# Third sum two pairs of steps sooner, standard chunks kept apart, activation sums in three steps, first loads one by one

## The chip, the cores and the metric

The kernel runs on one core of one Trainium2 chip. The metric is the device time of one execution in microseconds (us). The median of three runs before the change is 2226.44 us, from 2221.94 to 2226.76.

## What is computed

A block of a streaming encoder, float32, 256 frames of 2048 channels: half an FFN, two token mixers side by side (attention over chunks and retention) with gates, half an FFN again, and a final norm. The FFNs are the part that this change touches.

```python
def rmsnorm(x, g):
    y = x * lax.rsqrt(jnp.mean(x * x, axis=-1, keepdims=True) + EPS)
    return y * g

def swiglu_ffn(x, w_gate, w_up, w_down):      # 2048 -> 5632 -> 2048
    return (jax.nn.silu(x @ w_gate) * (x @ w_up)) @ w_down

x = x + 0.5 * swiglu_ffn(rmsnorm(x, g1), w1_gate, w1_up, w1_down)
...
x = x + merged @ w_out
x = x + 0.5 * swiglu_ffn(rmsnorm(x, g2), w2_gate, w2_up, w2_down)
return rmsnorm(x, norm_final_g)
```

## The kernel before

**One product in three matmuls.** Every float32 operand is split into hi (rounded to the matmul's own format, a copy on ACT, line 119) and lo (the rest, a subtraction on DVE, line 120). `three` (lines 127 to 129) adds hi x hi, hi x lo and lo x hi into one PSUM bank. A matmul has 128x128 weights and 512 columns.

**Steps.** The whole program is a list of steps, written out when the kernel is built. A standard step (a "chunk", `standard`) takes 2 x 128 rows of one weight matrix by 512 columns: SP loads 512 KB into one of 4 raw tiles, ACT and DVE split them, and PE does 12 matmuls (2 row blocks x 2 halves of the frames x 3). `run` emits for step c first the preparation (`prep`) of up to four steps ahead of it, then what `later` has made due at step c, then the products of step c. Engines are in order, so this order of emission is the order on each engine; they wait for each other by semaphores alone, and an engine with nothing to wait for runs ahead of the others.

**The groups.** In each FFN, 2 of the 11 blocks of 512 hidden columns are done with standard steps (`plain`), the other 9 as a `Strassen` group, which computes gate and up of one block with seven half-size products in place of eight. It works on sums: x and k are tiles of 512 KB that POOL's queue loads (line 495; at most 8 at a time, `KEPT`), x from gate's weights and k from up's. A group has four phases with four positions jc each. Phases 0, 1 and 2 have pairs of half steps ("r", of a plain tile, and "s", of a sum), phase 3 has four single half steps; a half step has 6 matmuls. In order:

- phase 0: x += k (DVE, line 526); split k (r), then x (s)
- phase 1: SP loads a raw tile of gate; x += raw (line 531); split raw (r), then x (s)
- phase 2: SP loads a raw tile of up; k = x - k (the third sum, line 533); POOL issues a transfer that adds a tile of up's weights to x while it writes (the accumulating transfer, line 534, 512 KB); split raw (r), then k (s)
- phase 3: split x (s)

Once k is prepared in phase 2 and x in phase 3, their room goes to the next group's loads, which POOL's queue issues in between. Groups are named in the trace by the number of their first step: z12, z51, z89, z128, z166, z205, z243, z281, z320 in the first FFN and z624, z663, z701, z740, z778, z817, z855, z893, z932 in the second. A tile's name has the phase, the position and r or s at the end: `hiz16633s` is hi of z166, phase 3, jc 3, sum.

**Chunks between the half steps.** The order is made in `ffn`. After a lead of 12 chunks, groups run in sequence, and every pair (a quarter of it for the singles of phase 3) adds `rate`, about 0.80, to a credit. While the credit is at least 0.6 (0.2 at the end of a phase) a chunk of the queue follows, if what it reads is at hand. So there are mostly three or four chunks in a phase and one in phase 3. Where a job had to wait for its input, the credit grows over 1 and two chunks follow each other: six times in each FFN. Most chunks are of `down`, where each job's banks are first seeded with x on ACT (line 673) and emptied on ACT (line 676); two of those six double chunks go across from one such job to the next.

**The activations.** `Norm.put` transposes x and splits it. For the groups, `add_up` makes four further sums (s5, s6, s3, s7) for each half of the channels: DVE adds into a tile n1f or n2f (lines 444 to 453), then ACT makes hi (line 407) and DVE lo (408). They are due 1, 3, 5 and 7 steps after the last `put` of the half. 1/rms is made of the squares by DVE (line 336) and POOL (line 337); SiLU of the first plain block (f1g, f2g, line 635) needs it.

**Other work that lies in POOL's queue.** The bias table of the attention (biasT, line 313) is loaded 24 steps ahead of the mixers' first step, that is within phase 2 of z320; PE turns it (psb, line 323) four steps later.

Of the kernel before, what the change touches and what calls it, by code (L numbers as in the profile page):

```python
# [8 lines left out]
F32 = mybir.dt.float32  # L9
F32R = mybir.dt.float32r  # L10
AF = mybir.ActivationFunctionType
ALU = mybir.AluOpType
# [15 lines left out]
KC = 2  # L28
# [9 lines left out]
HALF_K = D // P // 2  # L38
LEAD = 12
SINGLE = 0.25  # L40
HELD = 6
PLAIN = (9, 10)
PASSES = ((9, 0), (10, 1), (2, 3), (4, 5), (6,), (7,), (8,))
WARM = (6, 3)
# [24 lines left out]
def block_kernel(ctx: ExitStack, tc: tile.TileContext, x, g1, w1g, w1u, w1d, gm, w_in, rel, woa, wor, wo,  # L69
                 g2, w2g, w2u, w2d, gf, cos, sin, decay, ident, out):  # L70
    nc = tc.nc
# [23 lines left out]
    steps = []  # L95
    transfers = []
    kept = []
# [4 lines left out]
    def later(n, fn):  # L102
        due.setdefault(state["step"] + n, []).append(fn)
# [4 lines left out]
    def chunk(w, r0, c0):  # L108
        return w[r0 : r0 + KC * P, c0 : c0 + NB].rearrange("(k p) n -> p k n", p=P)
# [5 lines left out]
    def split(raw, name, parts=(slice(0, KC),)):  # L115
        hi = wpool.tile([P, KC, NB], F32R, tag="hi", bufs=SPLIT_BUFS, name=f"hi{name}")
        lo = wpool.tile([P, KC, NB], F32R, tag="lo", bufs=SPLIT_BUFS, name=f"lo{name}")
        for p in parts:
            nc.scalar.copy(hi[:, p, :], raw[:, p, :])  # L119
            nc.vector.tensor_sub(lo[:, p, :], raw[:, p, :], hi[:, p, :].bitcast(F32))  # L120
        return hi, lo
# [250 lines left out]
    class Norm:  # L372
# [25 lines left out]
                if self.sums:  # L398
                    nc.vector.tensor_scalar_mul(self.minus, self.rstd, -1.0)

        def split_to(self, key, js, src):
            if key not in self.part:
                self.part[key] = [
                    apool.tile([P, HALF_K, P], F32R, tag="act", name=f"{self.name}{key}{i}") for i in "hl"
                ]
            hi, lo = self.part[key]
            nc.scalar.copy(hi[:, js, :], src)
            nc.vector.tensor_sub(lo[:, js, :], src, hi[:, js, :].bitcast(F32))

        def put(self, b, half):  # L410
            if half == 0:
                self.raw[b] = act_tile(F32, f"{self.name}x{b}")
            raw = self.raw[b]
            ps = side_tile(f"{self.name}p{b}{half}")
            for i in range(2):
                k = 4 * b + 2 * half + i
                for t in range(NT):
                    nc.tensor.transpose(
                        ps[:, (2 * i + t) * P : (2 * i + t + 1) * P], xs[t][:, k * P : (k + 1) * P], id_sb
                    )  # L420
            for i in range(2):
                k = 4 * b + 2 * half + i
                nc.scalar.activation(
                    raw[:, 2 * half + i, :], ps[:, i * SEQ : (i + 1) * SEQ], AF.Copy, scale=self.gain[:, k : k + 1]
                )
            j = 4 * (b // 2) + 2 * half
            for t in range(NT):
                src = raw[:, 2 * half : 2 * half + 2, t * P : (t + 1) * P]
                self.split_to(f"a{t}{b % 2}", slice(j, j + 2), src)
            if half == 1 and not self.sums:  # L430
                del self.raw[b]
            elif half == 1 and b % 2 == 1:
                for i, key in enumerate(self.SUMS):
                    later(1 + 2 * i, lambda key=key: self.add_up(b // 2, key))

        def add_up(self, p, key):

            a11, a21, a12, a22 = [self.raw[2 * p + i][:, :, t * P : (t + 1) * P] for i in range(2) for t in range(NT)]
            if key == "s5":
                f = act_tile(F32, f"{self.name}f{p}").rearrange("p a (h q) -> p h a q", h=2)  # L440
                self.f[p] = f[:, 0], f[:, 1]
            f0, f1 = self.f[p]
            if key == "s5":
                nc.vector.tensor_sub(f0, a22, a21)
                src = f0
            elif key == "s6":
                nc.vector.scalar_tensor_tensor(f1, f0, -1.0, a11, op0=ALU.mult, op1=ALU.subtract)
                src = f1
            elif key == "s3":
                nc.vector.scalar_tensor_tensor(f0, f1, -1.0, a12, op0=ALU.mult, op1=ALU.subtract)  # L450
                src = f0
            else:
                nc.vector.tensor_sub(f1, a11, a21)
                src = f1
                del self.raw[2 * p], self.raw[2 * p + 1], self.f[p]
            self.split_to(key, slice(4 * p, 4 * p + 4), src)

        def __call__(self, k, t):
            b = k // 4
# [12 lines left out]
    class Strassen:  # L472
# [37 lines left out]
        def step(self, phase, jc, of_sum):  # L510
            made = {}
            name = f"{self.name}{phase}{jc}{'rs'[of_sum]}"
            n = HALF_K // KC

            def load():
                made["raw"] = weights_tile(f"raw{name}")
                i = 2 - phase
                fetch(made["raw"], self.w[i], self.rows(1, jc), self.col[i])

            def prep():  # L520
                x = self.x[jc]
                if not of_sum:

                    k = self.kept[jc]
                    if phase == 0:
                        nc.vector.tensor_add(x, x, k)
                        made["w"] = split(k, name)
                        return
                    raw = made.pop("raw")
                    if phase == 1:  # L530
                        nc.vector.tensor_add(x, x, raw)
                    else:
                        nc.vector.tensor_sub(k, x, k)
                        nc.gpsimd.dma_start(x, chunk(self.w[0], self.rows(1, jc), self.col[0]), accum_op=ALU.add)
                    made["w"] = split(raw, name)
                elif phase == 2:
                    made["w"] = split(self.kept.pop(jc), name)
                elif phase == 3:
                    made["w"] = split(self.x.pop(jc), name)
                else:  # L540
                    made["w"] = split(x, name)

            bank, form, fresh, closing = {
# [4 lines left out]
            }[phase, of_sum]  # L548

            def products():  # L550
                hi, lo = made["w"]
                if fresh and jc == 0:
                    self.bank(bank)
                for i in range(KC):
                    three(
                        self.acc[bank], self.norm.form(form, KC * jc + i), (hi[:, i, :], lo[:, i, :]),
                        fresh and jc == 0 and i == 0, closing and jc == n - 1 and i == KC - 1, True,
                    )
                if jc == n - 1:
                    self.end(phase, of_sum)  # L560

            loaded = not of_sum and phase in (1, 2)
            frees = ["raw"] if loaded else ["kept"] if of_sum and phase > 1 else []
            return Step(self, 0, load if loaded else None, prep, frees, products)
# [53 lines left out]
    def ffn(name, norm, wg, wu, wd, after):  # L618
# [70 lines left out]
        first, second = [plain(b) for b in PLAIN]  # L689
# [8 lines left out]
        def next_standard():  # L698

            job, k = queue[0]  # L700
            if len(queue) <= apart or any(at_hand.get(b, len(steps) + 1) > len(steps) for b in job.needs):
                return False
            steps.append(standard(job, k))
            del queue[0]
            if job.makes is not None and k + KC == job.nk:
                at_hand[job.makes] = len(steps) + 5
            return True

        for _ in range(LEAD):
            next_standard()  # L710
        groups = [b for b in range(nblocks) if b not in PLAIN]
        pairs = 3 * (HALF_K // KC)
        rate = (len(queue) - apart) / (len(groups) * (pairs + SINGLE * HALF_K // KC))
        credit = 0.0
        for b in groups:
            group = paired(b)
            kept.extend((len(steps) - 10 if b == groups[0] else 0, fn) for fn in group.loads())
            for i, part in enumerate(group.steps()):
                steps.extend(part)
                credit += rate * (1 if i < pairs else SINGLE)  # L720
                if i + 1 == pairs + HALF_K // KC:
                    at_hand[b] = len(steps) + 6
                while credit >= (0.2 if (i + 1) % (HALF_K // KC) == 0 else 0.6) and next_standard():
                    credit -= 1
        for job, k in queue:
            steps.append(standard(job, k))
# [286 lines left out]
    def at(step, fn):  # L1013
        due.setdefault(step, []).append(fn)
# [119 lines left out]
```

## Time and profile before

| what | us |
|---|---|
| median of 3 runs | 2226.44 |
| the profiled execution | 2227.66 |
| its span, first to last instruction | 2225.9 |
| nine groups of the first FFN (66.4 to 743.5) | 677.1 |
| mixers and the projection after them (743.5 to 1483.5) | 740.0 |
| nine groups of the second FFN (1520.9 to 2173.9) | 653.0 |

The profile page gives busy time and share of the span for each engine (PE is TensorE, PEld its weight loads, DVE VectorE, ACT ScalarE, POOL GpSimd; SPq and POOLq are the queues that issue transfers). Rows of the table by stretches have the stretch and its length, then busy us with the count of instructions for PE, PEld, DVE, ACT and POOL, then the granted clock of TensorE (1 is full), the busy share of the 16 DMA engines, and GB/s. Rows of a timeline have start, duration, engine, source line, operation, tiles as out<-in, and in brackets how long the engine was idle before it and what ended that. Rows of waits have who waited for whom: total us, times, longest.

### The profile page before, as it was taken

How to read it: one execution, taken by the hardware profiler on the slowest of the kernel's cores; microseconds unless marked ns; L12 is line 12 of the kernel's file. 1: busy time of each engine (PE TensorE's matmuls, PEld its weight loads, DVE VectorE, ACT ScalarE, POOL GpSimd, SP SyncE). 2: the span in 40 equal slices, each digit the busy share in tenths (PEclk: the TensorE clock that was granted, in tenths of full speed). 3: DMA queues.
4: the chain of work that ended last, by engine and by line, in shares of the span. 5: the costliest groups of instructions: out<-in, count | busy, mean ns of one | idle time of the engine just before them, and what ended most of it. 6: DMA issues, size and time to landing. Idle time of an engine off the chain costs nothing.

```text
span 2225.9 us, 25616 instructions
## 1 busy us (share of the span) xinstructions
PE 2127.7 (96%) x9376; PEld 1730.3 (78%) x9376; DVE 1629.9 (73%) x1678; ACT 1325.5 (60%) x1648; POOL 215.2 (10%) x252
## 2 busy tenths in 40 slices
PE   7998999999999899999999999999999999999998
PEld 5776877787778788888888888887778777877786
DVE  4987988898888554555665554568889888888886
ACT  6565666676667664455444444556666566766675
POOL 1012101110111000000000000010111011101200
PEclk9999999999999999999999999999999999999999
DMA  7479657866786656656556666565787578767874
GB/s 256 120 230 284 193 181 234 263 189 191 232 249 170 200 177 183 189 163 178 170 161 191 192 194 190 187 231 159 227 265 207 173 227 254 201 191 223 263 193 147
DMA packets 214669, 452.27 MB, mean 203 GB/s; under 512 B 14016, under 2 KB 14768, under 8 KB 214544
## 3 DMA queue, kind: packets, MB, share of 16 engines
q1 hardware_dynamic: 172256, 331.39, 47.9%
q0 software_dynamic: 42144, 119.19, 18.9%
q8 instruction: 73, 1.20, 0.2%
q14 instruction: 52, 0.43, 0.1%
q10 hardware_dynamic: 144, 0.07, 0.0%
HBM read 446.92 MB, written 3.67 MB: 202 GB/s over the span
## 4 chain that ended last, share of the span: by engine, by line
PE 59%; issue 13%; DMA 11%; DVE 7%; ACT 7%; POOL 2%; ACTq 0%; SPq 0%; POOLq 0%; DVEq 0%
PE acc L128 15%; PE acc L129 15%; PE acc L127 15%; DVE lo L120 2%; ACT hi L119 2%; DMA raw<-in_ffn_w_down_dram 1%; DMA raw<-in_ffn_w_gate_dram 1%; DMA z205x<-in_ffn_w_gate_dram 1%; DMA z855x<-in_ffn_w_gate_dram 1%; DMA z663x<-in_ffn_w_gate_dram 1%; DMA z243x<-in_ffn_w_gate_dram 1%; DMA z740x<-in_ffn_w_gate_dram 1%; DMA z51k<-in_ffn_w_up_dram 1%; DMA gf<-in_norm_final_g_dram 1%; DMA z51x<-in_ffn_w_up_dram 1%
## 5 line engine op out<-in xcount | busy, mean ns | idle before, releaser
L120 DVE TENSOR_TENSOR lo<-raw,hi 128x1024 fp32r<-128x1024 f32 (+1 forms) x481 | 584.7, 1221 | 397.0 <-ACT hi L119 394.9
L119 ACT CAST hi<-raw 128x1024 fp32r<-128x1024 f32 (+1 forms) x481 | 503.1, 1049 | 357.1 <-PE acc L129 305.9
L127 PE MATMUL acc<-hi,nma00h 128*128 128x512 f32 x176 | 70.6, 401 | 0.0
L127 PE MATMUL acc<-hi,nma01h 128*128 128x512 f32 x176 | 70.1, 398 | 0.0
L129 PE MATMUL acc<-hi,nma00l 128*128 128x512 f32 x176 | 68.7, 390 | 0.0
L129 PE MATMUL acc<-hi,nma01l 128*128 128x512 f32 x176 | 68.6, 390 | 0.0
L127 PE MATMUL acc<-hi,nma10h 128*128 128x512 f32 x176 | 68.6, 390 | 0.0
L128 PE MATMUL acc<-lo,nma00h 128*128 128x512 f32 x176 | 68.6, 390 | 0.0
L128 PE MATMUL acc<-lo,nma01h 128*128 128x512 f32 x176 | 68.6, 390 | 0.0
L127 PE MATMUL acc<-hi,nma11h 128*128 128x512 f32 x176 | 68.6, 390 | 0.0
L129 PE MATMUL acc<-hi,nma10l 128*128 128x512 f32 x176 | 68.6, 390 | 0.0
L129 PE MATMUL acc<-hi,nma11l 128*128 128x512 f32 x176 | 68.6, 390 | 0.0
L128 PE MATMUL acc<-lo,nma10h 128*128 128x512 f32 x176 | 68.5, 389 | 0.0
L128 PE MATMUL acc<-lo,nma11h 128*128 128x512 f32 x176 | 68.5, 389 | 0.0
L673 ACT ACTIVATE acc<-xall 128x512 f32<-128x512 f32 x96 | 57.5, 599 | 7.0 <-DVE f2g L640 2.8
L676 ACT ACTIVATE xall<-acc 128x512 f32<-128x512 f32 x96 | 55.9, 585 | 2.5 <-PE acc L129 2.5
L127 PE MATMUL acc<-hi,mgh 128*128 128x512 f32 x128 | 50.1, 392 | 0.0
L129 PE MATMUL acc<-hi,mgl 128*128 128x512 f32 x128 | 49.8, 389 | 0.0
L128 PE MATMUL acc<-lo,mgh 128*128 128x512 f32 x128 | 49.8, 389 | 0.0
L337 POOL TENSOR_TENSOR rs<-v,mhalf 128x4 f32<-128x4 f32 x4 | 4.0, 1010 | 369.0 <-DVE v L336 369.0
L129 PEld LDWEIGHTS acc<-hi,nma10l 128*128 128x128 f32 x176 | 33.1, 188 | 7.0
L129 PEld LDWEIGHTS acc<-hi,nma00l 128*128 128x128 f32 x176 | 33.0, 188 | 7.0
(4907 smaller groups left out, 6434.0 us busy)
## 6 DMA issues: line engine op xcount, KB each, us to landing
raw<-in_ffn_w_down_dram SPq DMA_DIRECT2D x176, 512.0 KB, 5.4
raw<-in_w_in_dram SPq DMA_DIRECT2D x176, 512.0 KB, 3.7
raw<-in_ffn_w_up_dram SPq DMA_DIRECT2D x32, 512.0 KB, 6.0
raw<-in_w_out_dram SPq DMA_DIRECT2D x32, 512.0 KB, 3.8
raw<-in_ffn_w_gate_dram SPq DMA_DIRECT2D x31, 512.0 KB, 5.0
raw<-in_w_out_att_dram SPq DMA_DIRECT2D x16, 512.0 KB, 4.0
raw<-in_w_out_ret_dram SPq DMA_DIRECT2D x16, 512.0 KB, 4.0
z12k<-in_ffn_w_up_dram POOLq DMA_DIRECT2D x4, 512.0 KB, 10.9
```

The costliest lines, as they stand in the source:

```text
L119: nc.scalar.copy(hi[:, p, :], raw[:, p, :])
L120: nc.vector.tensor_sub(lo[:, p, :], raw[:, p, :], hi[:, p, :].bitcast(F32))
L127: nc.tensor.matmul(acc, ahi, whi, start=first, stop=False, **more)
L128: nc.tensor.matmul(acc, ahi, wlo, start=False, stop=False, **more)
L129: nc.tensor.matmul(acc, alo, whi, start=False, stop=last, **more)
L337: nc.gpsimd.tensor_tensor(dst, v, mhalf[:, :width], op=ALU.pow)
L673: nc.scalar.activation(acc, xs[t][:, cols], AF.Copy, scale=2.0)
L676: nc.scalar.activation(xs[t][:, cols], acc, AF.Copy, scale=0.5)
```

## The change

1. The third sum and its accumulating transfer of position jc were issued in phase 2 at position jc. They now are issued `AHEAD_THIRD` = 2 pairs sooner: those of jc 0 and 1 in phase 1 at positions 2 and 3, those of 2 and 3 in phase 2 at positions 0 and 1. Within the step they now come behind the split of the raw tile, not ahead of it.
2. `while` becomes `if`: after a pair at most one chunk follows. Each of the six double chunks of an FFN is pulled apart; its second one comes behind the next pair (or, in phase 3, behind the second single).
3. The sums of the activations are due 1, 4, 7 and 10 steps after the last `put`, and hi and lo of each no longer follow in the same step, but 1 and 2 steps after the sum.
4. The eight loads of an FFN's first group, all due at step 2 of its lead, become due one by one at steps 3 to 10.

```diff
+AHEAD_THIRD = 2
...
             elif half == 1 and b % 2 == 1:
                 for i, key in enumerate(self.SUMS):
-                    later(1 + 2 * i, lambda key=key: self.add_up(b // 2, key))
+                    later(1 + 3 * i, lambda key=key: self.add_up(b // 2, key))
...
-            self.split_to(key, slice(4 * p, 4 * p + 4), src)
+            hi, lo = [x[:, 4 * p : 4 * p + 4, :] for x in self.pair(key)]
+            later(1, lambda: nc.scalar.copy(hi, src))
+            later(2, lambda: nc.vector.tensor_sub(lo, src, hi.bitcast(F32)))
...
+            def third(at):
+
+                x, k = self.x[at], self.kept[at]
+                nc.vector.tensor_sub(k, x, k)
+                nc.gpsimd.dma_start(x, chunk(self.w[0], self.rows(1, at), self.col[0]), accum_op=ALU.add)
+
...
                     raw = made.pop("raw")
                     if phase == 1:
                         nc.vector.tensor_add(x, x, raw)
-                    else:
-                        nc.vector.tensor_sub(k, x, k)
-                        nc.gpsimd.dma_start(x, chunk(self.w[0], self.rows(1, jc), self.col[0]), accum_op=ALU.add)
                     made["w"] = split(raw, name)
+                    at = (phase - 1) * n + jc - AHEAD_THIRD
+                    if 0 <= at < n:
+                        third(at)
...
-            kept.extend((len(steps) - 10 if b == groups[0] else 0, fn) for fn in group.loads())
+            first = len(steps) - 9 if b == groups[0] else 0
+            kept.extend((first + i if first else 0, fn) for i, fn in enumerate(group.loads()))
...
-                while credit >= (0.2 if (i + 1) % (HALF_K // KC) == 0 else 0.6) and next_standard():
+                if credit >= (0.2 if (i + 1) % (HALF_K // KC) == 0 else 0.6) and next_standard():
                     credit -= 1
```

More of the change, by code (lines that the diff above doesn't have):

```diff
@@ L399, in square, with pair @@
                     nc.vector.tensor_scalar_mul(self.minus, self.rstd, -1.0)
-        def split_to(self, key, js, src):
+        def pair(self, key):
             if key not in self.part:
@@ L405, in split_to @@
                 ]
-            hi, lo = self.part[key]
+            return self.part[key]
+        def split_to(self, key, js, src):
+            hi, lo = self.pair(key)
             nc.scalar.copy(hi[:, js, :], src)
@@ L522, in prep @@
                 if not of_sum:
-                    k = self.kept[jc]
                     if phase == 0:
-                        nc.vector.tensor_add(x, x, k)
-                        made["w"] = split(k, name)
+                        nc.vector.tensor_add(x, x, self.kept[jc])
+                        made["w"] = split(self.kept[jc], name)
                         return
```

## The prediction

> **What bounds the kernel now.** I read the page's first part, then the time table by stretches, then the timeline of TensorE and the list of its waits.
>
> ```profile
> span 2225.9 us, 25616 instructions
> PE 2127.7 (96%) x9376; PEld 1730.3 (78%) x9376; DVE 1629.9 (73%) x1678; ACT 1325.5 (60%) x1648; POOL 215.2 (10%) x252
> ```
>
> TensorE is called busy 96% of the span, but matmuls overlap, so its pitch is the better measure. The timeline of PE shows it: these two rows are the first and the last of 27 matmuls in a row.
>
> ```profile
> 428.71 0.39 PE L127 MATMUL acc<-hi,f1a1h 128*128 128x512 f32 x1
> ...
> 434.62 0.39 PE L129 MATMUL z166a<-hiz16632s,n1a11l 128*128 128x512 f32 x1
> ```
>
> So one matmul per 5.91/26 = 0.2273 us. A half step (6 matmuls) is worth 1.36 us, a standard chunk (12) 2.73 us. The two stretches with the nine groups of each FFN follow, in the table by stretches (length, then PE, PEld, DVE, ACT and POOL busy with counts, granted clock, DMA share, GB/s).
>
> ```profile
> 66.40:743.50 677.10, 635.87 (x2728) 509.98 (x2728) 565.82 (x521) 434.89 (x508) 101.34 (x115) 0.97 0.71 214
> 1520.90:2173.90 653.00, 625.05 (x2710) 504.07 (x2709) 560.71 (x508) 431.27 (x501) 92.96 (x104) 0.99 0.72 215
> ```
>
> At that pitch 2728 and 2710 instructions are at most 620 and 616 us (some are shorter transposes): at least 57 and 37 us are lost there. Where, the same table cut by phases tells: z166 is one group (phases 1, 2, 3), then phases 1 and 3 of the next.
>
> ```profile
> 389.20:411.10 21.90, 21.90 (x98) 17.96 (x97) 20.38 (x19) 15.33 (x18) 2.71 (x3) 1.00 0.68 202
> 411.10:430.80 19.70, 19.64 (x86) 15.61 (x85) 16.01 (x15) 12.61 (x15) 7.42 (x10) 1.00 1.07 296
> 430.80:443.20 12.40, 9.31 (x38) 6.61 (x37) 7.11 (x8) 6.65 (x9) 0.58 (x1) 1.00 0.98 345
> ...
> 463.90:482.90 19.00, 19.00 (x85) 15.74 (x84) 17.70 (x16) 13.24 (x16) 1.97 (x2) 1.00 0.65 189
> ...
> 502.60:518.00 15.40, 12.02 (x38) 8.30 (x37) 9.43 (x9) 5.71 (x7) 0.51 (x1) 0.78 0.91 306
> ```
>
> Phase 3 of z166 holds four half steps and one chunk, 36 matmuls or 8.18 us, and takes 12.4; that of z205 takes 15.4, at a clock of 0.78. Phase 1 loses nothing. The reason stands in the timeline, at the last accumulating transfer of z166 (DVE makes the third sum, POOL issues the transfer, ACT then makes hi of x, DVE lo).
>
> ```profile
> 421.29 1.22 DVE L533 TENSOR_TENSOR z166k<-z166x,z166k 128x1024 f32<-128x1024 f32 x1
> 422.82 1.21 POOL L534 DMA_DIRECT2D z166x<-in_ffn_w_up_dram  x1 [2.21 <-DVE z166k L533]
> 434.72 1.05 ACT L119 CAST hiz16633s<-z166x 128x1024 fp32r<-128x1024 f32 x1 [2.29 <-DMA z166x<-in_ffn_w_up_dram]
> 435.80 1.23 DVE L120 TENSOR_TENSOR loz16633s<-z166x,hiz16633s 128x1024 fp32r<-128x1024 f32 x1 [3.62 <-ACT hiz16633s L119]
> ```
>
> The transfer needs 11.9 us from issue to use. ACT, DVE and PE are in order, so everything prepared behind it is late too, and the lead of four prepared steps is gone. That stall ends phase 3 of most groups, and it is what the change aims at.
>
> **The change part by part.** First, the third sum two pairs sooner. Per group 4 subtractions and 4 transfers move, none is added. For the price of phase 3 once the transfers are in time I take phases of this very trace: z243 and z855 have no chunk in phase 3 (5.46 us at the pitch), and z663 has one ahead of its last half step, which gives its transfer time. The last row sums all 16 phase 3 stretches of the groups that have another behind them.
>
> ```profile
> 583.60:589.10 5.50, 5.50 (x25) 4.51 (x25) 3.81 (x5) 3.66 (x5) 0.00 (x0) 1.00 0.90 339
> ...
> 1653.00:1662.00 9.00, 8.55 (x38) 6.57 (x36) 6.14 (x7) 5.54 (x9) 0.00 (x0) 1.00 1.05 363
> ...
> 2027.40:2032.80 5.40, 5.40 (x25) 4.48 (x24) 3.71 (x5) 3.69 (x5) 0.00 (x0) 1.00 0.92 348
> ...
> sum 191.20, PE 154.09 PEld 110.80 DVE 112.66 ACT 87.27 POOL 11.16; mean PE 9.63 PEld 6.93 DVE 7.04 ACT 5.45 POOL 0.70
> ```
>
> Without these three rows 13 stretches take 191.2 - 19.9 = 171.3 us, against 13 x 8.18 = 106.3: 65 us lost. z663 shows 9.0 - 8.2 = 0.8 us of loss with a transfer in time. At 0.8 each, 15 stretches (the two without a chunk get one) keep 12 of 65: **-53 us**. Is two pairs enough? A pair is 2.73 us and its chunk 2.73, so the issue comes about 2 x 5.4 = 10.9 us sooner, against 2.29 us for which ACT waited here; the sum needs only x and k of a pair that was prepared two pairs before. What is late next is DVE's add for c22 in front of SiLU and the next hi, which z663's 0.8 holds already. I count lost matmuls and not PE's idle time, 191.2 - 154.1 = 37 us, since the row with 0.78 shows that a stall slows the matmuls behind it too. The Trainium skill, "TensorE: Matmul & The Clock Gate", "Part 1: The HAM clock gate", has the half rate come after an idle window of about 3.4 us; by it these shorter gaps would cost their idle time alone, and the term would be nearer 37 less 12, -25 us. The trace differs, since the longest single wait in that stretch was 2.0 us (z205a, below).
>
> Two of the four moved subtractions now fall into phase 1, behind hi and lo of a raw tile, the other two into the first half of phase 2. Two rows in order on DVE give the pitch of one:
>
> ```profile
> 394.41 1.22 DVE L531 TENSOR_TENSOR z166x<-z166x,rawz16612r 128x1024 f32<-128x1024 f32 x1
> 395.55 1.22 DVE L120 TENSOR_TENSOR loz16612r<-rawz16612r,hiz16612r 128x1024 fp32r<-128x1024 f32 x1
> ```
>
> 1.14 us; two in phase 1 make 2.3. Phase 1 of z205 has 17.7 busy in 19.0 us, so 20.0 would be wanted, 1.0 over, and phase 2, which loses two, has room (16.0 of 19.7 before). Cover is the lead of four steps, 5.4 us of PE; gone, the cost is 2.3 x 18 = 41 us. Bounds 0 and 41. I take 6: nothing where chunks stand between the pairs, 1.5 us in each of the four groups where pairs 2 and 3 of phase 1 follow each other bare: **+6 us**. ACT gains: its hi of k in phase 2 no longer waits for DVE's subtraction; I count nothing.
>
> Second, the chunks in a row, the waits for seeds, and the rest of the waits that the change touches (the list of waits: total, times, longest).
>
> ```profile
> PE psb L323 <- DMA biasT<-rel_ext: 7.3, 1, 7.3
> PE acc L127 <- ACT acc L673: 6.8, 4, 2.8
> PE acc L127 <- ACT f1g L635: 4.9, 1, 4.9
> ...
> PE acc L127 <- ACT n1a01h L407: 3.7, 4, 2.2
> ...
> PE z205a L127 <- ACT hiz20533s L119: 2.0, 1, 2.0
> PE acc L127 <- ACT f2g L635: 1.9, 1, 1.9
> ```
>
> The 6.8 us are where two chunks in a row cross from one down job to the next: ACT has to seed the new banks while PE stands. Two half steps, 2.73 us of PE, now stand between, against a longest wait of 2.8: **-6.5 us**; bounds 0 and -7. The other chunks that are pulled apart change no sum, only the lead, and are in the range.
>
> The 7.3 us are the bias table: its transfer stands in POOL's queue behind the last accumulating one.
>
> ```profile
> 708.15 1.22 POOL L534 DMA_DIRECT2D z320x<-in_ffn_w_up_dram  x1 [4.38 <-DVE z320k L533]
> ...
> 719.44 1.20 POOL L534 DMA_DIRECT2D z320x<-in_ffn_w_up_dram  x1 [3.46 <-issue]
> 720.17 2.04 POOL L313 DMA_DIRECT2D biasT<-rel_ext  x2
> ```
>
> Now the last is issued where the second was, 11.3 us sooner. If the two tiles are free by then, nearly all 7.3 goes; if they are those that k leaves in phase 2, nothing does. I take **-5**. POOL's other queue members (the next group's loads) stand behind the same or an earlier event; SP's queue gets no instruction.
>
> Third, the sums of the activations, taken apart into three steps. POOL has 1/rms ready at 48.5; ACT is then held by DVE's sums:
>
> ```profile
> 47.75 0.73 POOL L337 TENSOR_TENSOR n1rstd<-v,mhalf 128x2 f32<-128x2 f32 x1 [39.86 <-DVE v L336]
> ...
> 49.31 0.62 ACT L407 CAST n1s3h<-n1f 128x512 fp32r<-128x512 f32 x1 [2.11 <-DVE n1f L450]
> ...
> 53.22 1.27 ACT L635 ACTIVATE f1g<-acc,n1rstd 128x512 f32<-128x512 f32 x2
> ```
>
> Both copies that stood there are due later, so SiLU (f1g) can start near 49.1 instead of 53.2: -4.1. In the second FFN the 1.9 of f2g goes the same way, and of the 3.7 of n1a01h 1.5, as one such copy stood ahead: **-7.5 us**, bounds 0 and -10.5. Fourth, the spread first loads: POOL runs ahead of the program (the 39.86 us above are its wait for that 1/rms, all eight loads issued before), so five of the eight still go at once and three fall behind it. The early 3.7 us wait for x ends before those three matter: 0, bounds -4.6 (three at 1.5 us) and 0.
>
> One gain more, in phase 0, where DVE now catches up after each stall; here that of z205:
>
> ```profile
> 443.20:463.90 20.70, 20.19 (x94) 16.59 (x93) 20.60 (x20) 14.17 (x18) 0.00 (x0) 1.00 0.30 92
> ```
>
> DVE has 20.6 of 20.7 us busy. The eight half steps and three chunks are 84 matmuls, 19.1 us, and eight short transposes at half the pitch 0.9, so some 0.7 us is lost, 12 in 18 groups. With DVE ahead I take **-4**, bounds 0 and -8.
>
> Sum: -53 + 6 - 6.5 - 5 - 7.5 - 4 = -70. The profiled execution took 2227.7 us (span 2225.9), 1.2 over the median of 2226.4, so 2226.4 - 70 = **2156 us**.
>
> **The rivals.** The rows of transfers (KB each, median us to landing) carry the one on the other side.
>
> ```profile
> z166x<-in_ffn_w_gate_dram POOLq DMA_DIRECT2D x4, 512.0 KB, 12.0
> z166x<-in_ffn_w_up_dram POOLq DMA_DIRECT2D x4, 512.0 KB, 11.2
> ...
> rawz16613r<-in_ffn_w_gate_dram SPq DMA_DIRECT2D x1, 512.0 KB, 3.7
> ...
> rawz16623r<-in_ffn_w_up_dram SPq DMA_DIRECT2D x1, 512.0 KB, 8.5
> ```
>
> (1) Slower: a raw load takes 3.7 us in phase 1 and 8.5 at the end of phase 2, where the engines are full (share 1.07). The moved transfers take this crowd to four pairs from phase 1 on. SP prefetches four raw tiles, two pairs or 10.9 us. From a landing of 10.9 on PE waits for raws; at POOL's 12.0 each of four pairs loses 1.1, 4.4 per group, 79 in 18 groups, more than the 70: 2235 us. Against it: phase 1 moves 189 to 202 GB/s, two transfers of 0.52 MB in 19 us add 55, and phase 2 showed 296. The Trainium skill, "DMA: Bandwidth & Descriptors", "Issuing engines are not separate DMA queues", says that transfers from all issuers interleave on the same 16 engines; by it lateness is only handed on, and the trace agrees so far that raws slow beside POOL's.
>
> (2) DVE becomes the bound in phase 1: the full 41 instead of 6, 2156 + 35 = 2191 us. For it: 20.38 of 21.9 busy.
>
> (3) The transfer isn't sooner, since POOL is held by something in phase 2: only the seeds and the activation sums remain, 2226 - 14 = 2212 us.
>
> (4) More: nothing is left of phase 3, DVE costs nothing, phase 0 gives 8, the bias table 7: 2156 - 12 - 6 - 4 - 2 = 2132 us.
>
> **How the numbers follow.** Forecast 0.60, (4) 0.13, (2) 0.13, (3) 0.04, (1) 0.08, and 0.02 for a mixture that ends near no change. The range, 2130 to 2198, takes the forecast with its bounds, (4) and (2). Faster by over 0.2% (about what a measurement of this kernel tells from no change) 0.89, the same 0.03, slower 0.08.
>
> **What would show it.** Right: phase 3 with one chunk near 9 us at clock 1.00, ACT's hi of x with no wait for a transfer, f1g near 49 us, the seed wait gone from the list, DVE over 19 us busy in phase 1 with PE whole. Wrong: ACT waiting for raws around phase 2, DVE lo as PE's releaser in phase 1, a bias wait as long as before.

## The result, and the profile after

| | before, us | after, us |
|---|---|---|
| median (4 runs each) | 2226.6 (2221.9 to 2231.1) | 2188.3 (2184.0 to 2189.4) |
| the profiled execution | 2227.66 | 2189.41 |
| its span | 2225.9 | 2187.0 |
| nine groups of the first FFN | 677.1 | 659.0 |
| nine groups of the second FFN | 653.0 | 646.3 |

After over before is 0.9825, with an interval of 0.980 to 0.985: 38 us less, where 70 were forecast. The direction and the range held; the size is a little over half.

The first lines of the page after:

```profile
span 2187.0 us, 25642 instructions
PE 2108.5 (96%) x9376; PEld 1714.6 (78%) x9376; DVE 1618.8 (74%) x1678; ACT 1314.8 (60%) x1648; POOL 214.6 (10%) x252
```

Nothing in them tells what happened: every engine has the work that it had. The table by stretches does. First the two FFNs, then z166 in its phases 1, 2 and 3, then phase 3 of z205, and the sum over the 16 phase 3 stretches.

```profile
54.50:713.50 659.00, 625.67 (x2726) 502.05 (x2725) 563.04 (x526) 430.45 (x509) 101.07 (x115) 0.99 0.73 220
1489.30:2135.60 646.30, 622.16 (x2710) 499.61 (x2710) 558.52 (x511) 428.21 (x504) 92.71 (x104) 1.00 0.73 218
...
380.20:399.70 19.50, 19.50 (x85) 15.60 (x84) 19.14 (x18) 12.84 (x15) 2.55 (x3) 1.00 0.79 208
399.70:423.60 23.90, 22.57 (x97) 17.86 (x97) 16.77 (x16) 14.64 (x19) 7.52 (x10) 1.00 1.04 333
423.60:433.60 10.00, 8.78 (x37) 6.68 (x37) 7.13 (x8) 6.54 (x9) 0.63 (x1) 1.00 0.73 255
...
494.60:503.30 8.70, 8.50 (x37) 6.68 (x36) 6.77 (x8) 5.05 (x6) 0.27 (x1) 1.00 0.97 350
...
sum 149.90, PE 142.53 PEld 111.44 DVE 112.37 ACT 92.56 POOL 9.03; mean PE 8.91 PEld 6.96 DVE 7.02 ACT 5.78 POOL 0.56
```

Phase 3 of z205 has the same work as before and takes 8.7 us at clock 1.00, where it took 15.4 at 0.78. The 16 phase 3 stretches took 191.2 us and take 149.9. Phase 1 of z166 keeps PE whole, with DVE busy for 19.14 of 19.5 us. Phase 2 of z166 has become the loser: its 8 half steps and 4 chunks are 96 matmuls, 21.8 us at the pitch, and it takes 23.9. (A phase can hold another number of chunks than before, so stretches of one phase are compared with their own matmuls, not with each other.)

The hi of x that waited 2.29 us for its transfer before has no bracket any more, so it waited for nothing:

```profile
404.62 1.20 POOL L530 DMA_DIRECT2D z166x<-in_ffn_w_up_dram  x1 [3.06 <-DVE z166k L529]
...
425.15 1.03 ACT L120 CAST hiz16633s<-z166x 128x1024 fp32r<-128x1024 f32 x1
```

This is the list of PE's waits after (total us, times, longest).

```profile
PE acc L129 <- DVE lo L121: 21.0, 31, 5.3
PE f1a9p L347 <- DVE gains L263: 4.8, 1, 4.8
...
PE acc L128 <- ACT f1g L646: 2.0, 1, 2.0
PE f2a10p L347 <- DVE f2g L651: 1.6, 1, 1.6
PE f1a10p L347 <- DVE f1g L651: 1.6, 1, 1.6
...
PE psb L324 <- ACT bias L329: 1.3, 1, 1.3
```

The seed wait (6.8 before) isn't in the list, the bias wait is 1.3 instead of 7.3 and f1g's 2.0 instead of 4.9. New are `gains` (4.8), f1g and f2g as tiles made by DVE (1.6 each), and a lo that came 5.3 us late.

**Where the time went.** PE's idle time leaves out that matmuls behind a stall run slower (in phase 3 of z205 before, eight of them start 0.43 us apart in place of 0.227), so I count lost time as the prediction did: for each matmul of the profiled execution the time to the start of the next, less 0.227 us (0.11 for a short transpose), summed by phase over all 18 groups. "Lead" is what comes ahead of an FFN's first group.

| us lost | lead 1 | lead 2 | phase 0 | phase 1 | phase 2 | phase 3 | between | sum |
|---|---|---|---|---|---|---|---|---|
| before | 26.9 | 3.8 | 12.6 | 1.8 | 37.2 | 66.8 | 6.8 | 155.8 |
| after | 15.0 | 1.8 | 14.6 | 15.2 | 49.4 | 14.7 | 6.7 | 117.4 |
| change | -11.9 | -2.0 | +2.0 | +13.4 | +12.2 | -52.1 | -0.1 | -38.4 |

The sums differ by 38.4 us and the spans by 38.9, so the table accounts for the result. In phase 2 two gains hide part of a loss. z320, where the bias table is waited for, goes from 11.1 to 2.9; z243 and z855, where the seeds were waited for, from 9.7 together to 1.9. The other 15 groups go from 16.4 to 44.5. So phase 3 gave all that was forecast, and phases 1 and 2 took back 13.4 + 28.1 = 41.5 us beside those gains, where the sum had +6.

### The profile page after: what moved, and what is told of

It reads as the page before. It is cut to its first block, busy times and chain, and to the rows that moved or that the text cites. A ratio compares the mean times of both kernels' runs of the same rounds, so it can differ in the third digit from the quotient of the medians.

```text
span 2187.0 us, 25642 instructions
## 1 busy us (share of the span) xinstructions
PE 2108.5 (96%) x9376; PEld 1714.6 (78%) x9376; DVE 1618.8 (74%) x1678; ACT 1314.8 (60%) x1648; POOL 214.6 (10%) x252
## 5 line engine op out<-in xcount | busy, mean ns | idle before, releaser
L684 ACT ACTIVATE acc<-xall 128x512 f32<-128x512 f32 x96 | 57.4, 598 | 11.2 <-DVE f2g L651 4.9
L129 PEld LDWEIGHTS acc<-lo,nma10h 128*128 128x128 f32 x176 | 33.1, 188 | 7.0
```

What stands on the lines that cost most here:

```text
L129: nc.tensor.matmul(acc, ahi, wlo, start=False, stop=False, **more)
L684: nc.scalar.activation(acc, xs[t][:, cols], AF.Copy, scale=2.0)
```

## The experiments

Two theories went in. **D**: the moved subtractions hold DVE up, and what stands behind them is late. **L**: the moved transfers slow the raw loads, and ACT waits for those. Each edit is against the kernel after unless it says before. Times are medians; the ratios are to runs of the kernel before on the same chip, with medians from 2223.0 to 2226.1, while it was 2226.6 beside the result: up to 3.6 us of a difference to the kernel after can come from there. Kernel 3 is that of experiment 3, and so on.

**1. The third sum alone** (before, with `third` and its new place).

```diff
+AHEAD_THIRD = 2
...
-                    else:
-                        nc.vector.tensor_sub(k, x, k)
-                        nc.gpsimd.dma_start(x, chunk(self.w[0], self.rows(1, jc), self.col[0]), accum_op=ALU.add)
                     made["w"] = split(raw, name)
+                    at = (phase - 1) * n + jc - AHEAD_THIRD
+                    if 0 <= at < n:
+                        third(at)
```

> The kernel before with the third sum two pairs sooner and nothing else of the change. Theory D (order on DVE and ACT: the two subtractions that fall into phase 1 make DVE late, the sum for c12 comes late, SiLU on ACT waits for it and the next hi waits behind SiLU) and theory L (the moved transfers crowd the raw loads, ACT waits for raws) both expect phase 3 to lose under 1.5 us a group instead of 4.1, and some 25 to 30 us of that given back in phases 1 and 2: 2200 us, from 2192 to 2210. If the giving back comes from the chunks pulled apart instead, 2175 us or less.

2194.1 us, ratio 0.987 (0.985 to 0.989): -29. As expected. In its trace phase 3 loses 11.8 in place of 66.8 and the bias wait is 1.3, while the waits for seeds stay (6.9 in all): the bias table belongs to the third sum, the seeds don't. Phase 1 loses 13.4 and the 15 groups of phase 2 lose 32.2. So 27.4 of the 41.5 us taken back come with the third sum alone, and the other edits add 14.1 on top of it.

**2. The third sum back in its position, but still behind the split.**

```diff
-AHEAD_THIRD = 2
+AHEAD_THIRD = 4
```

> The kernel after with the third sum and its transfer back at its old position (AHEAD_THIRD 4, still behind the split of the raw tile). Both theories: phase 3 loses 4 us a group again, phases 1 and 2 lose as little as before; what stays is the lead (14 us by the two traces) and the seeds (7): 2205 us, from 2198 to 2212.

2259.5 us, ratio 1.017 (1.015 to 1.019): slower than before by 36, and a miss by 55. Phase 2 alone loses 100.9 us. The order on the engines tells why, here in z701:

```profile
1724.39 1.22 DVE L529 TENSOR_TENSOR z701k<-z701x,z701k 128x1024 f32<-128x1024 f32 x1
...
1725.72 1.05 ACT L120 CAST hiz70120s<-z701k 128x1024 fp32r<-128x1024 f32 x1 [2.72 <-DVE z701k L529]
```

The next thing that ACT has to do is hi of this k. With the subtraction behind the split, DVE makes lo of the raw tile first, which itself needs ACT's hi of that tile, and then k; ACT stands 2.72 us for it here. In all it waits 60 times and 161.3 us for such a k, where it did 29 times and 47.8 us before. This says that the place within the step matters as soon as the sum is needed in the same pair, and that the kernel isn't the one for "all but the third sum". That is the next.

**3. All but the third sum**, which is where it was, ahead of the split.

```diff
+                    else:
+                        third(jc)
                     made["w"] = split(raw, name)
-                    at = (phase - 1) * n + jc - AHEAD_THIRD
-                    if 0 <= at < n:
-                        third(at)
```

> The kernel after with the third sum and its transfer exactly as before the change, at phase 2's own position and ahead of the split. Against third_back this tells what the place behind the split costs there: if the 36 us over the kernel before come from hi of k waiting for the subtraction behind lo, 2204 us here, from 2197 to 2211; if the chunks pulled apart and the sums cost them, 2250 us or more.

2202.1 us, ratio 0.991 (0.988 to 0.994): -22, as expected, and 57 less than the last. So the third sum, added to the other edits, brings 2202.1 - 2188.3 = 14 us (19 by the two ratios), half to two thirds of what it brings alone.

**4. `if` for `while` alone** (before).

```diff
-                while credit >= (0.2 if (i + 1) % (HALF_K // KC) == 0 else 0.6) and next_standard():
+                if credit >= (0.2 if (i + 1) % (HALF_K // KC) == 0 else 0.6) and next_standard():
```

> The kernel before with only the chunks pulled apart (if for while). The wait for seeds of 6.8 us should go; nothing else moves by more than 3 us: 2219 us, from 2214 to 2224. The wait of the first transposes for the gains' copy (4.8 us in the kernel after) shows here if it comes from the order of the chunks, and not if it comes from DVE's load in phase 1.

2217.4 us, ratio 0.997 (0.996 to 0.998): -5.6. The size held and the wait for seeds is gone, but that nothing else moves by more than 3 us was wrong: phase 3 falls from 66.8 to 49.6 (most in z740, from 5.8 to 0.1, where a chunk now stands behind the first half step), phase 1 rises from 1.8 to 5.9, all of it in z12, and 15 groups in phase 2 (all but z243, z320, z855) from 16.4 to 24.0. The wait for `gains` is there too:

```profile
PE f1a9p L346 <- DVE gains L262: 3.8, 1, 3.8
```

So that wait comes from the new order of the chunks; by what way, this run doesn't tell.

**5. The activation sums alone** (before, with the first and second hunks of the diff; the first loads stay at step 2).

> The kernel before with only the sums of the activations taken apart (due 1, 4, 7, 10, hi and lo one and two steps later); the first loads are all at step 2 as before. The sums' theory: the lead loses 15 to 17 us instead of 27 and the second lead 1.8 instead of 3.8, 2214 us, from 2211 to 2217. If the spread of the first loads made part of the lead's gain, less: 2219 us.

2214.5 us, ratio 0.997 (0.995 to 0.999): -8.5, as expected in the time. Lead 1 loses 19.0, against 26.9 before, where 15 to 17 were expected, and 14.8 in kernel 3, which has the spread loads too. One thing was not looked for: the double chunks stand here as before, and yet PE hardly waits for seeds, 1.5 us in place of 6.8, and z243 and z855 lose nothing in phase 2.

```profile
PE acc L127 <- ACT acc L678: 1.5, 2, 0.7
```

**6. A small subtraction.** The third sum is made on 8 of 512 columns; the instruction, its waits and its transfer stay.

```diff
-                nc.vector.tensor_sub(k, x, k)
+                nc.vector.tensor_sub(k[:, :, 0:8], x[:, :, 0:8], k[:, :, 0:8])
```

> The kernel after with the third subtraction on 8 of 512 columns only (16 of 1024 elements of each partition); the rest of k keeps its old values. Every order and wait stays, DVE loses some 1.1 us four times a group. Theory D: SiLU's wait for c12 falls from over 3 us to about 2, the stalls in phases 1 and 2 go back to what they were before the change, 2163 us, from 2155 to 2172. Theory L: the raws are as late as ever, 2185 us or more.

2169.2 us, ratio 0.974 (0.972 to 0.976): 19 below after. D was close in the time, L wrong. The instruction went from 1.22 to 0.17 us; phase 1 loses 6.1 instead of 15.2, the 15 groups in phase 2 35.1 instead of 44.5: 18.5 together. D had these stalls go back to what they were before the change (1.8 and 16.4), and they went less than half of the way.

**7. A small transfer**: 64 KB instead of 512, from the same place.

```diff
-                nc.gpsimd.dma_start(x, chunk(self.w[0], self.rows(1, at), self.col[0]), accum_op=ALU.add)
+                nc.gpsimd.dma_start(x[:, 0:1, 0:P], chunk(self.w[0], self.rows(1, at), self.col[0])[:, 0:1, 0:P], accum_op=ALU.add)
```

> The kernel after with the accumulating transfer on 128 of the 1024 columns of a tile only, 64 KB instead of 512 KB; DVE's work and every order stay. Theory L: ACT's waits for raw loads of down and up fall from 40 us to under 10 and the stalls of phases 1 and 2 with them, 2163 us, from 2155 to 2172. Theory D: those waits fall too, but PE's time hardly does, 2180 us or more.

2175.3 us, ratio 0.977 (0.975 to 0.979): 13 below after, between what D and L expected. So both are real. Phase 1 stays at 16.3; the 15 groups in phase 2 lose 32.5, 12.0 less. ACT's wait for the raw tiles of down shows what the transfers do (with those of up it falls from 40.2 to 25.1 us, where L had expected under 10); in the list of waits of before, of after and of this kernel, in this order:

```profile
ACT hi L119 <- DMA raw<-in_ffn_w_down_dram: 9.4, 9, 2.1
```

```profile
ACT hi L120 <- DMA raw<-in_ffn_w_down_dram: 29.5, 17, 4.1
```

```profile
ACT hi L120 <- DMA raw<-in_ffn_w_down_dram: 11.4, 8, 2.4
```

**8. One pair sooner instead of two.**

```diff
-AHEAD_THIRD = 2
+AHEAD_THIRD = 3
```

> The kernel after with the third sum one pair sooner than before the change instead of two (AHEAD_THIRD 3). One subtraction falls into phase 1 instead of two. Theory D: half of DVE's excess, phase 3 still in time (one pair is some 5 us, the transfers were up to 4.9 us late), 2178 us. Theory L: the transfers lie where the raws were latest before, phase 2 as late as now, 2190 us.

2169.5 us, ratio 0.974 (0.972 to 0.976): 19 below after, and faster than both theories expected. One subtraction falls into phase 1 instead of two: that loses 8.4 instead of 15.2, phase 2 40.7 instead of 49.4, and phase 3 only 10.8. So one pair is lead enough for the transfer. The second pair gained at one place alone, the bias table (PE's wait for it is 3.6 us here, 1.3 with two pairs), and cost more than that elsewhere.

**9. SiLU of c12 and c22 two steps later.** Both D and the wait for c22 that the prediction named led here. This is c12 in z166 of the kernel after, in the timeline:

```profile
403.10 1.22 DVE L529 TENSOR_TENSOR z166k<-z166x,z166k 128x1024 f32<-128x1024 f32 x1
404.23 0.74 DVE L591 SCALAR_TENSOR_TENSOR z166c<-z166c,n1minus,z166c 128x512 f32<-128x512 f32 x1
405.01 0.63 ACT L664 ACTIVATE z166c<-z166c 128x512 f32<-128x512 f32 x1 [3.09 <-DVE z166c L591]
405.55 1.03 ACT L120 CAST hiz16621s<-z166k 128x1024 fp32r<-128x1024 f32 x1
406.61 1.23 DVE L121 TENSOR_TENSOR loz16621s<-z166k,hiz16621s 128x1024 fp32r<-128x1024 f32 x1 [1.64 <-ACT hiz16621s L120]
407.89 0.50 PE L129 MATMUL z166a<-loz16621s,n1s7h 128*128 128x512 f32 x1 [0.76 <-DVE loz16621s L121]
```

Each row releases the next. ACT has nothing to do for 3.09 us, because SiLU of c12 stands at its head and its sum is queued on DVE behind a subtraction; the hi behind SiLU needs only k. DVE then waits 1.64 us for that hi, and PE 0.76 for lo. In before SiLU waits here too, 1.96 us, and with the small subtraction 2.04:

```profile
412.71 0.63 ACT L653 ACTIVATE z166c<-z166c 128x512 f32<-128x512 f32 x1 [1.96 <-DVE z166c L580]
```

```profile
397.42 0.63 ACT L664 ACTIVATE z166c<-z166c 128x512 f32<-128x512 f32 x1 [2.04 <-DVE z166c L591]
```

```diff
+SILU = 2
...
-                    self.evict(0, 1, r)
+                    later(SILU, lambda: self.evict(0, 1, r))
...
-                    self.evict(1, 1, r)
+                    later(SILU, lambda: self.evict(1, 1, r))
```

> The kernel after with SiLU of c12 and of c22 due two steps after the sums that they read, so that ACT makes the next hi first. Theory D: the waits of ACT for c12 and c22 go, with them most first stalls of phase 2, 2172 us, from 2165 to 2180. Theory L: no more than 4 us faster.

2152.7 us, ratio 0.967 (0.965 to 0.969): 36 below after, twice what D expected. ACT's 36 waits for these sums, 92.8 us in after, are 0.9 in all. Its timeline in z166:

```profile
394.21 1.05 ACT L121 CAST hiz16621s<-z166k 128x1024 fp32r<-128x1024 f32 x1
397.13 1.05 ACT L121 CAST hi<-raw 128x1024 fp32r<-128x1024 f32 x1 [1.87 <-DMA raw<-in_ffn_w_down_dram]
398.08 0.63 ACT L665 ACTIVATE z166c<-z166c 128x512 f32<-128x512 f32 x1
```

hi comes ahead of SiLU, and SiLU waits for nothing. Phase 2 loses 35.4 instead of 49.4, phase 3 1.6 instead of 14.7 and phase 0 3.6 instead of 14.6; phase 1 stays at 15.8. The edit thus works in other phases than the subtractions of phase 1 do, so it may be a bound of its own. The same edit on the kernel before tells.

**10. The same on before.**

> The kernel before with SiLU of c12 and c22 due two steps after their sums and nothing of the change. If the waits for SiLU cost only where DVE is loaded by the moved subtractions, under 8 us faster, since phase 3 still ends with the late transfer: 2218 us. If they were a bound of their own before the change: phases 0 and 2 lose 15 to 20 us less, phase 3 stays near 65 us of loss, 2207 us, from 2200 to 2212.

2189.8 us, ratio 0.985 (0.982 to 0.989): -34, more than either reading expected (under 8, and 17 with the range ending at 2200). That the waits were a bound of their own is the nearer one, but its places were wrong in part: phase 2 loses 16.4 less, as expected, phase 0 doesn't lose less (13.2, 12.6 before), and phase 3, which was to stay near 65, falls from 66.8 to 46.7. ACT's 36 waits for c12 and c22, 75.2 us in before, are gone from the list. To put SiLU later was worth about as much before (34) as after (36), so the change neither made this bound nor took it away. Alone it brings nearly as much as the whole change.

**11. One pair sooner, and SiLU later** (8 and 9 together).

> The kernel after with both: SiLU two steps later and the third sum one pair sooner than at first instead of two. Theory D alone (DVE's order was all that the second pair cost): no faster than silu_later by more than 4 us, 2150 us. If the late raws of phase 2 (some 20 us of loss there in silu_later) come from the transfers moved into phase 1, they shrink: 2141 us, from 2134 to 2147.

2139.2 us, ratio 0.962 (0.959 to 0.966): as the late raws were expected to give, and faster than D alone expected. By the medians it is 49 below after, a little less than the two gains added (55). Phase 2 loses 25.6 instead of 35.4 in kernel 9, phase 1 8.0 instead of 15.8. But the edit moves a transfer and a subtraction together, so it doesn't tell which of them phase 2 gained by.

**12. The two single collisions moved as well**: the gains turned from step 24 on instead of 28 (the second FFN's from 40 on instead of 48), and the copies of the bias table (`rel`) four steps later.

```diff
-        later(6, lambda: spread_rel(tiles))
+        later(10, lambda: spread_rel(tiles))
...
-        at(20 * i, lambda i=i, g=g: later(8, load_gain(g, i)))
+        at(16 * i, lambda i=i, g=g: later(8, load_gain(g, i)))
```

> silu_one with two collisions taken apart: the gains of the mixers' norm are turned at step 24 instead of 28, where the first block's transposes wait for them (a wait of 4.7 us), and the bias table's copies on DVE are due 10 instead of 6 steps after their loads (DVE stood still there and PE waited 4.6 us). Both waits should go from the list: 9 us faster than silu_one, 2135 us.

2133.9 us, ratio 0.960 (0.957 to 0.964): 90 below before, 54 below after by the medians, 49 by the ratios. PE's list of waits has no `gains` any more and its longest wait for lo is 0.8 us (3.8 and 4.1 in kernel 11):

```profile
PE acc L130 <- DVE lo L122: 6.7, 13, 0.8
...
PE psb L325 <- DMA biasT<-rel_ext: 3.1, 2, 2.9
```

But 9 us over experiment 11 were expected, and the five found lie within that one's interval (0.003 either way, or 7 us), so only the lost time of single phases carries the two edits: z12's phase 1 goes from 6.0 to 0.5 us and z51's phase 2 from 6.7 to 2.5, while z320's phase 2 rises from 4.3 to 6.4.

The lost time of these kernels, counted as above; the sum also holds the 6.7 us between the FFNs' stretches. It is of one profiled execution each, which can be some us off the median: `if` alone and the sums alone lose 15.0 and 16.5 us less than before by this count and were 5.6 and 8.5 faster in time.

| us lost | lead 1 | lead 2 | phase 0 | phase 1 | phase 2 | phase 3 | sum |
|---|---|---|---|---|---|---|---|
| third sum alone | 26.0 | 1.9 | 15.3 | 13.4 | 46.2 | 11.8 | 121.3 |
| all but the third sum | 14.8 | 1.7 | 12.8 | 5.8 | 38.8 | 50.4 | 131.1 |
| `if` alone | 26.9 | 1.9 | 13.6 | 5.9 | 36.1 | 49.6 | 140.8 |
| activation sums alone | 19.0 | 1.5 | 12.8 | 2.0 | 28.0 | 69.3 | 139.3 |
| small subtraction | 16.0 | 1.5 | 14.8 | 6.1 | 39.4 | 13.4 | 98.0 |
| small transfer | 17.6 | 1.5 | 14.4 | 16.3 | 37.3 | 10.0 | 103.8 |
| one pair sooner | 16.5 | 1.5 | 14.8 | 8.4 | 40.7 | 10.8 | 99.4 |
| SiLU later | 14.9 | 4.2 | 3.6 | 15.8 | 35.4 | 1.6 | 82.2 |
| before, SiLU later | 27.6 | 1.5 | 13.2 | 1.7 | 20.8 | 46.7 | 118.2 |
| 11 | 16.4 | 1.5 | 4.4 | 8.0 | 25.6 | 1.7 | 64.4 |
| 12 | 16.4 | 1.5 | 7.5 | 2.7 | 24.1 | 2.3 | 61.2 |

## Why the prediction was right in direction and too large in size

**Third sum, -53 in phase 3: this step held.** Phase 3 lost 52.1 us less, by the mechanism named: the hi of x has no wait for a transfer any more and the clock stays at 1.00. The third sum alone does all of it (kernel 1: from 66.8 to 11.8). `if` alone and SiLU later alone take 17 and 20 us of the same loss with the transfers where they were (kernels 4 and 10), so these gains overlap and can't be added. To count lost matmuls and not idle time was right as well: PE's idle time in the 16 stretches fell by only 30 us, from 37.1 to 7.4.

**Subtractions on DVE, +6: right in the one place it priced; what it put at nothing failed.** The four groups in which pairs 2 and 3 of phase 1 follow each other bare are z89, z128, z701 and z740. They lose 1.1, 2.3, 1.0 and 2.3 us in phase 1 after, 6.7 together, and 0.4 with a small subtraction: the 6 came where it was expected. Three things that stood at nothing in the sum cost most of the rest. Phase 2 "has room" was wrong, the chunks that are pulled apart "change no sum" was wrong, and the slowing of raw loads by the moved transfers was weighed as a rival alone. The runs show in place of the 6:

| | us | from |
|---|---|---|
| the order of the chunks, `if` | +11.7 | kernels 4 and 3 against before: phase 1 +4.1, 15 groups of phase 2 +7.6 |
| the moved subtractions | +18.5 | small subtraction: phase 1 9.1, phase 2 9.4 |
| the moved transfers | +12.0 | small transfer: phase 2 |
| together | +42.2 | against 41.5 found |

The first row is what an edit adds to before, the other two what an edit takes from after, so that they sum so closely is in part luck; kernel 1 splits the same 41.5 into 27.4 for the third sum and 14.1 for the rest.

In phase 1 the lead does cover most of the subtraction where chunks stand between: z166 loses 0.5 there, z205 0.3. The largest loss of phase 1, z12's 6.9, is 5.8 with a small subtraction too and 5.8 with `if` alone: it is the order of the chunks, not the subtraction. Half of the 18.5 is in phase 2, where I had said that DVE "has room": it has, 16.77 of 23.9 us, but its queue is in order, and the sum for c12 stands in it behind a subtraction while ACT stands with SiLU at its head. Busy time can't show this; ACT's bracket shows it, 1.96 us before, 3.09 after, 2.04 with a small subtraction, and so do its 36 waits for c12 and c22 in all, 75.2, 92.8 and 71.6 us. That a subtraction delays c12 is shown by these; how much of the 9.4 us goes by this way, and how much by a later lo, no run separates.

**What is late next.** The prediction named c22's add in front of SiLU and held that z663's 0.8 us contained it. It was the next bound, with c12 beside it, and worth 34 to 36 us in whichever kernel. Since it is worth about the same before and after, it explains little of what the forecast lost; it is a gain that the forecast didn't see.

**Double chunks and seeds, -6.5.** The seed wait is gone from the list, and z243 and z855 lose 7.8 less: right in size. The cause is shown only in part. `if` alone takes the wait away (kernel 4), but it also nearly goes where the double chunks stay: 1.5 us in kernel 5 and 1.8 in kernel 10, where z243 and z855 together lose 0.5 or less. So two chunks in a row don't suffice for it; what else it needed wasn't followed. That pulling the other chunks apart "changes no sum" was wrong by the 11.7 above on one side and the 17 of phase 3 on the other.

**Bias table, -5.** 7.3 became 1.3, z320 lost 8.2 less: right; that it is the third sum's doing is shown by kernel 1 (1.3) and kernel 3 (7.2). With one pair less (kernel 8) it is 3.6.

**Activation sums, -7.5; first loads, 0.** The sums alone were timed at -8.5, and f1g starts at 48.14 there, near the 49 forecast. In the kernel after it starts earlier still. In the timeline of after, POOL's 1/rms between two rows of ACT:

```profile
42.23 0.60 ACT L461 CAST n1s6h<-n1f 128x512 fp32r<-128x512 f32 x1
42.87 0.73 POOL L338 TENSOR_TENSOR n1rstd<-v,mhalf 128x2 f32<-128x2 f32 x1 [37.16 <-DVE v L337]
...
44.14 1.26 ACT L646 ACTIVATE f1g<-acc,n1rstd 128x512 f32<-128x512 f32 x2
```

1/rms itself is at 42.87 instead of 47.75. From there to f1g it took 5.5 us before and takes 1.3: that is the 4.1 forecast for lead 1. The earlier 1/rms comes with the spread loads. In the kernels without them it is made at 46.87 (kernel 5) to 48.45 (kernel 10), in those with them at 42.76 (kernel 3) to 44.49 (kernel 2). Kernel 3 has all but the third sum:

```profile
42.76 0.73 POOL L338 TENSOR_TENSOR n1rstd<-v,mhalf 128x2 f32<-128x2 f32 x1 [37.05 <-DVE v L337]
```

Lead 1 loses 19.0 without them in kernel 5, and 14.8 to 17.6 in the kernels that have both. So they are worth 1.4 to 4.2 us, within the bound of -4.6, and not 0. My reason, that the early wait for x ends before they matter, doesn't hold: PE's transposes of x end sooner too, the last one starting at 33.78 instead of 37.06 (36.95 in kernel 5). The spread loads alone weren't tried, but neither of the two other edits in kernel 3 has that effect by itself (kernels 4 and 5).

**Phase 0, -4.** It lost 2 us more, not 4 less. That DVE is no longer late from phase 3 wasn't enough: phase 0 falls, to 3.6, only where the third sum is sooner and SiLU is later too (kernel 9). Either alone leaves it at 13 to 15 (kernels 10 and 1).

**The rivals.** (1) was real in its mechanism and wrong in its price: the raw tiles do come late. In the rows of transfers after, and in the timeline of z166:

```profile
rawz16623r<-in_ffn_w_up_dram SPq DMA_DIRECT2D x1, 512.0 KB, 11.3
```

```profile
414.57 1.05 ACT L120 CAST hiz16623r<-rawz16623r 128x1024 fp32r<-128x1024 f32 x1 [2.85 <-DMA rawz16623r<-in_ffn_w_up_dram]
```

11.3 us is beyond the 10.9 from which I had PE wait; ACT's waits for raw tiles of all kinds went from 24.2 to 79.4 us in all. But with up to four prepared steps in between, little of that reached PE: the price was 12 us, not 79. In kernel 12 these waits are 101.4 us, and that kernel is the fastest. (2) put DVE's bound at the whole 41; by chance the three costs add up to the same, but the subtractions are 18.5 of it, and phase 1, which it was about, shows only 9.1 of that. (3) is excluded by the transfer's issue, 4.9 us into phase 2 after and 11.7 before, and (4) took the +6 for too much where it was too little.

**What stays open.** Phase 2 still loses 24 us in kernel 12, and ACT still waits 101 us in all for raw tiles; whether more of these tiles would take that away wasn't tried. Why `if` costs 7.6 us in phase 2, and why SiLU later on the kernel before takes 20 us off phase 3, no run separates. Why lead 2 falls from 3.8 to between 1.5 and 1.9 also in kernels whose edits don't touch it (1 and 4), wasn't followed.

## What to carry to other kernels

When a stall is taken away by moving work sooner, price the places that it moves into not by the busy share of the engine but by what stands behind it in that engine's queue, and behind that in the next engine's. An instruction that needs another engine's fresh result, at the head of an in-order queue, holds up all that is ready behind it: making it due a few steps later cost nothing here and gave nearly as much as the change itself. And move no farther than the wait is long: one pair was enough, and the second cost 19 us in all.

## What the hardware showed that was not expected

In the prediction I read the share of 1.07 at 296 GB/s in phase 2 as full DMA engines. The last of the phase 3 stretches after has nearly the same share and moves more (as z663's row of before did, 363 at 1.05), and the accumulating transfers land sooner where they are spread:

```profile
2058.70:2067.40 8.70, 8.50 (x38) 6.68 (x37) 6.89 (x8) 5.08 (x6) 0.36 (x1) 1.00 1.04 387
```

```profile
z166x<-in_ffn_w_gate_dram POOLq DMA_DIRECT2D x4, 512.0 KB, 9.4
z166x<-in_ffn_w_up_dram POOLq DMA_DIRECT2D x4, 512.0 KB, 8.2
```

387 GB/s at a share of 1.04: a full share was no ceiling of bytes at 296. The accumulating transfer went from 11.2 to 8.2 us and the plain load of gate from 12.0 to 9.4, with 512 KB each; the medians of the 18 groups are 9.7 and 8.1, 12.9 and 10.8. So in this kernel a transfer that accumulates took no longer than a plain one of the same size on the same queue. That what runs beside a transfer makes it slow is borne out by the small transfers of kernel 7, with which the plain loads of gate, still 512 KB, take 7.8 (median of the 18 groups) instead of 10.8.
